# A two-block float32 transformer step on one core: the first job gets four column tiles, the first retention job runs ahead of its layer norm, and the last projection is computed token by column

## The chip, the cores and the metric

The kernel runs on one core of a Trainium2 chip. Times are device microseconds (us) of the whole program. A run is compared by the median of its executions; the profile shows one execution. TensorE is PE, VectorE DVE, ScalarE ACT, GpSimd POOL, and SyncE (SP) only starts transfers.

## The reference, cut to what matters

256 tokens of width 2048 pass through two blocks, all in float32. The parts that the change touches:

```python
h = rms_norm(x, norm_mix[l]); proj = h @ w_in[l]       # first block: four mixers side by side
kv = a_kv.reshape(B, T, 6, NSA_KV_HEADS, HEAD_DIM)      # kv[:, :, 0], kv[:, :, 1]: compressed keys and values
dq, dk, dv = jnp.split(d_cols, 3, axis=-1)              # of the stick-breaking attention
...
x = x + (silu(h @ w_ffn_gate[l]) * (h @ w_ffn_up[l])) @ w_ffn_down[l]
...
# second block: attention layer, then retention layer, each closed by
x = layer_norm(ALPHA * x + mixer(x), gain, bias)        # mean and variance over the 2048 columns of a token
# retention_mixer
proj = h @ w_in                                         # q, k (8 heads of 256), v, g (8 heads of 512)
q, k = rope(q), rope(k); o = chunk_retention(q, k, v, log_g, strict)
return (head_group_norm(o) * silu(g)) @ w_out           # 4096 -> 2048
```

The layer norm ahead of the retention is ln0 below, the one at the end ln1.

## The kernel before, in words

Activations are kept transposed: tile k holds columns 128k to 128k+127 on the partitions and the 256 tokens along the row. Every product is made of split operands: a value is a rounded part (hi) and the remainder (lo), both of a rounded float32 type. An activation tile is [hi | lo], 128x512 (names xA, xB, og, act). A weight unit is 128x1024, loaded by one SP transfer of 512 KB into wf (four buffers); ACT rounds it to wh (L374) and DVE subtracts, wl = wf - wh (L387). `prefetch` keeps wh three units and `low` keeps wl two units ahead of TensorE.

A job is one group of output columns over all rows of the weight. In a T job (`job_T`) the weights are stationary: each pair of a weight row block k and a column tile m takes one 512-column matmul with wh (hi and lo at once, L449) and one 256-column matmul with wl (L450); the result lies column by token. The variant `one` uses three 256-column matmuls (L446, L447, L450). In an N job (`job_N`) the activations are stationary, each row block and token half takes three 512-column matmuls (L473 to L475), and the result lies token by column.

The order of everything is written out: the body issues job after job, and between pairs `S.adv` lets a scheduler step the waiting tasks (generators), so that the evacuations, norms and attention parts are issued among the matmuls. Every engine works off its instructions in the order of issue. The jobs in order: kcvc, aq, ak, av, four dqk, dv, cv, ... (w_in), w_out, the FFN, then the attention's kv, q, g and four ao (output projection, four column tiles each), then for the retention rqk0 (q and k of head 0, four tiles), rv0, then rqk, rv and rg of the heads, and four ro (output projection).

Three places matter. At the **start** x arrives as eight transfers of 256 KB (two tiles each, xr) mixed with the weight units; each tile is scaled and split by ACT (L512) and DVE (L514).

At **ln0** the evacuation `ev_res` adds an ao tile to the residual (L1376, L1378). `LN.add` sums tiles 0 to 7 on POOL; that mean, spread by a matmul with ones (lp, L1293), is subtracted from every tile as a shift (L1297); `stat` squares the tiles on ACT (L1321) and adds them and their squares on POOL (L1322, L1324) into lns and lnq. `sums` adds over partitions by one-column matmuls (pcs, L1343), and `finish` takes mean, variance and rsqrt with some dozen small DVE operations, spreads them by matmuls with ones (lpb L1359, lpn L1367) and hands them to `apply0`, which normalises 16 tiles and splits them into x3 (xB tiles). Only then can rqk0 begin. The last ao job uses two additional buffers of wh and wl and the `one` form.

At the **end**, four T jobs ro feed ln1, which ends in the same `finish`; then the 16 tiles are normalised and leave in 16 transfers, as a 2048 x 256 array.

## Time and profile before

| | us |
|---|---|
| median of three runs | 2307.68 (2307.23 to 2321.01) |
| the profiled execution, own time | 2322.28 |
| its span, first to last instruction | 2320.5 |
| TensorE busy in the span | 2276.0 (98%) |
| VectorE / ScalarE / GpSimd busy | 1532.2 (66%) / 1141.5 (49%) / 414.8 (18%) |
| mean granted TensorE clock | 0.991 of full speed |
| DMA traffic | 408.55 MB, mean 176 GB/s |

The profiled execution lies 0.6% above the median and 0.05% above the slowest of the three runs. Busy time of TensorE comes from modelled ends, so the number of matmuls times the spacing of their starts says more than the 98%.

### The profile page before, as it was taken

How to read it: one execution, taken by the hardware profiler on the slowest of the kernel's cores; microseconds unless marked ns; L12 is line 12 of the kernel's file. 1: busy time of each engine (PE TensorE's matmuls, PEld its weight loads, DVE VectorE, ACT ScalarE, POOL GpSimd, SP SyncE). 2: the span in 40 equal slices, each digit the busy share in tenths (PEclk: the TensorE clock that was granted, in tenths of full speed). 3: DMA queues.
4: the chain of work that ended last, by engine and by line, in shares of the span. 5: the costliest groups of instructions: out<-in, count | busy, mean ns of one | idle time of the engine just before them, and what ended most of it. 6: DMA issues, size and time to landing. Idle time of an engine off the chain costs nothing.

```text
span 2320.5 us, 33510 instructions
## 1 busy us (share of the span) xinstructions
PE 2276.0 (98%) x12755; PEld 1963.9 (85%) x12755; DVE 1532.2 (66%) x2372; ACT 1141.5 (49%) x1690; POOL 414.8 (18%) x406
## 2 busy tenths in 40 slices
PE   8999999999999999999999999999999999999997
PEld 7877888888888888888888888888888888888887
DVE  6666697655555555555558898777677676776464
ACT  5457545544443344444445556455444544446343
POOL 2224331111100011110012222650000000001061
PEclk9999999999999999999999999989999999999998
DMA  7643455565565566666555454444655555556553
GB/s 251 227 150 112 122 187 180 195 190 187 182 192 188 177 189 189 188 185 191 183 190 181 146 156 153 156 168 160 185 168 175 179 172 187 169 173 189 188 168 114
DMA packets 114657, 408.55 MB, mean 176 GB/s; under 512 B 12882, under 2 KB 15186, under 8 KB 114368
## 3 DMA queue, kind: packets, MB, share of 16 engines
q1 hardware_dynamic: 113184, 400.80, 54.9%
q0 software_dynamic: 1168, 5.53, 0.7%
q8 instruction: 100, 1.64, 0.3%
q14 instruction: 61, 0.50, 0.1%
q10 hardware_dynamic: 144, 0.08, 0.0%
HBM read 404.24 MB, written 4.21 MB: 176 GB/s over the span
## 4 chain that ended last, share of the span: by engine, by line
PE 83%; DVE 5%; POOL 3%; issue 2%; ACT 1%; DMA 0%; POOLq 0%; ACTq 0%; DVEq 0%
PE st L449 41%; PE st L450 22%; PE st L473 5%; PE st L474 4%; PE st L475 4%; DVE wl L387 2%; POOL xr L1297 1%; PE mO L1809 1%; PE st L446 1%; PE st L447 1%; PE mA L854 1%; PE mS L1782 0%; POOL lnq L1324 0%; POOL lny L1649 0%; PE mO L835 0%
## 5 line engine op out<-in xcount | busy, mean ns | idle before, releaser
L387 DVE TENSOR_TENSOR wl<-wf,wh 128x1024 fp32r<-128x1024 f32 (+1 forms) x750 | 949.5, 1275 | 301.1 <-ACT wh L374 299.8
L374 ACT ACTIVATE wh<-wf 128x1024 fp32r<-128x1024 f32 (+1 forms) x750 | 788.4, 1055 | 698.9 <-PE st L449 440.9
L449 PE MATMUL st<-xA,wh 128*128 128x512 f32 x2144 | 768.3, 402 | 8.0 <-DVE xA L514 6.7
L450 PE MATMUL st<-xA,wl 128*128 128x256 f32 x2272 | 640.5, 282 | 2.8 <-DVE wl L387 2.8
L449 PE MATMUL st<-xB,wh 128*128 128x512 f32 x1536 | 548.7, 400 | 4.6 <-DVE xB L1655 2.1
L449 PEld LDWEIGHTS st<-xA,wh 128*128 128x128 f32 x2144 | 404.4, 189 | 107.5 <-DVE xA L514 6.7
L450 PEld LDWEIGHTS st<-xA,wl 128*128 128x128 f32 x2272 | 432.0, 190 | 4.2 <-DVE wl L387 4.1
L450 PE MATMUL st<-xB,wl 128*128 128x256 f32 x1536 | 432.0, 281 | 0.0
L449 PEld LDWEIGHTS st<-xB,wh 128*128 128x128 f32 x1536 | 290.4, 189 | 75.5 <-DVE xB L1655 3.2
L450 PEld LDWEIGHTS st<-xB,wl 128*128 128x128 f32 x1536 | 291.8, 190 | 1.1
L449 PE MATMUL st<-act,wh 128*128 128x512 f32 x704 | 248.8, 399 | 0.0
L450 PE MATMUL st<-act,wl 128*128 128x256 f32 x704 | 197.7, 281 | 0.0
L474 PE MATMUL st<-wl,xB 128*128 128x512 f32 x448 | 174.8, 390 | 1.0 <-DVE wl L387 1.0
L473 PE MATMUL st<-wh,xB 128*128 128x512 f32 x448 | 175.4, 392 | 0.0
L475 PE MATMUL st<-wh,xB 128*128 128x512 f32 x448 | 174.5, 389 | 0.0
L449 PEld LDWEIGHTS st<-act,wh 128*128 128x128 f32 x704 | 132.3, 188 | 33.1
L663 DVE TENSOR_TENSOR evs<-st,evt 128x256 f32<-128x256 f32 x110 | 46.2, 423 | 149.9 <-ACT evt L661 149.8
L450 PEld LDWEIGHTS st<-act,wl 128*128 128x128 f32 x704 | 133.0, 189 | 0.0
L1210 POOL TENSOR_TENSOR evs<-evs,R 128x256 f32<-128x256 f32 x44 | 32.4, 737 | 487.3 <-DVE evs L663 487.3
L1753 POOL TENSOR_TENSOR rm<-qkr,c 128x512 f32<-128x512 f32 x16 | 32.5, 2032 | 456.7 <-DVE qkr L1687 451.7
L474 PEld LDWEIGHTS st<-wl,xB 128*128 128x128 f32 x448 | 84.2, 188 | 17.9 <-DVE wl L387 1.9
L475 PEld LDWEIGHTS st<-wh,xB 128*128 128x128 f32 x448 | 84.1, 188 | 17.8
(426 smaller groups left out, 2604.8 us busy)
## 6 DMA issues: line engine op xcount, KB each, us to landing
wf<-in_w_c SPq DMA_DIRECT2D x264, 512.0 KB, 4.2
wf<-in_w_e SPq DMA_DIRECT2D x256, 512.0 KB, 3.9
wf<-in_w_d SPq DMA_DIRECT2D x112, 512.0 KB, 3.6
wf<-in_w_a SPq DMA_DIRECT2D x84, 512.0 KB, 3.8
wf<-in_w_b SPq DMA_DIRECT2D x32, 512.0 KB, 4.0
xr<-in_xT SPq DMA_DIRECT2D x16, 256.0 KB, 5.4
wf<-in_w_a SPq DMA_DIRECT2D x5, 420.0 KB, 4.1
dr<-d POOLq DMA_DIRECT2D x1, 2048.0 KB, 9.7
```

What stands on the lines that cost most here:

```text
L374: ACT.activation(wh[q][:, :n], wf[q][:, :n], AF.Copy)
L387: V.tensor_tensor(wl[q][:, :n], wf[q][:, :n], wh[q][:, :n].bitcast(F32), OP.subtract)
L446: PE.matmul(ps[m][:, :T], hv[:, cs], x[:, :T], start=kk == 0, stop=False)
L447: PE.matmul(ps[m][:, :T], hv[:, cs], x[:, T:], start=False, stop=False)
L449: PE.matmul(ps[m], hv[:, cs], x, start=kk == 0, stop=False)
L450: PE.matmul(ps[m][:, :T], lv[:, cs], x[:, :T], start=False, stop=kk == K - 1)
L473: PE.matmul(p, xh, h[:, o:o + n], start=kk == 0, stop=False)
L474: PE.matmul(p, xh, l[:, o:o + n], start=False, stop=False)
L475: PE.matmul(p, xl, h[:, o:o + n], start=False, stop=kk == K - 1)
L663: V.tensor_tensor(s, p[:, :T], t, OP.add)
L1210: G.tensor_tensor(s, s, R2, OP.mult)
L1753: G.tensor_tensor(m, x[:, ::-1], rsn.rearrange("p (a t) -> p a t", a=2), OP.mult)
```

## The change

**First job.** kcvc takes the first dqk job's two tiles with it: four tiles, two row blocks per unit (eight units in the place of four and four). Unit 0 is loaded and split in halves, and x's first transfer goes between its halves on the SP queue. Ten matmuls of ones stand at the head of TensorE's order. The splits of x from tile 6 on become a task.

**ln0 and rqk0.** The shift is the mean of the first four tiles (NS = 4), begun one job earlier. Each finished, not yet normalised tile is multiplied by its gain and split into xg = [hi | 4 columns | lo], where the four columns hold gain and bias, hi and lo. rqk0 multiplies xg (`ext`: 260, 256 and 258 columns), and its evacuation `ev_first` applies the norm to the four results: the first extra column sums give W·gain and W·bias, and with rm (rsqrt) and lpn (-mean·rsqrt) the result is W·xg·rm + (W·gain)·lpn + W·bias. `norm0` and `apply0` run as tasks beside rqk0; rv0 and the later jobs read the normalised x3. `one` and the additional buffers go. Closing phase 3 and loading c4 move into rv0's first evacuation. `decay` moves into the FFN.

**ro and the end.** The four ro jobs become N jobs, in the last one's last unit ordered by token half. The residual is added up, transposed (32 transposes) and copied by tasks; `bn_stats` runs on each 512 columns of a token half. The end has bn_aggr, rsqrt, 12 matmuls of ones, two transposes, six two-row matmuls that spread bias and mean term, and eight output transfers of 256 KB on two queues; the output is 256 x 2048.

```diff
-    job("a", "T", allk, [(w, cat([kv(0, g), kv(1, g)])) for g in range(2)], 4, "kcvc")
+    job("a", "T", allk, [(w, cat([kv(0, g), kv(1, g)])) for g in range(2)] + dq(0), 2, "kcvc")
...
-    for i in range(4):
-        dqk(i)
+    for i in (2, 1, 3):
+        job("a", "T", allk, dq(i), 4, ("dqk", i))
...
-        job("e", "T", rows, [("ret_w_out_2", P * (4 * m + j) + ar(P)) for j in range(4)], 2, ("ro", m))
+        job("e", "N", rows, [("ret_w_out_2", 512 * m + ar(512))], 2, ("ro", m))
...
+            for c in halves(q, n):
+                nc.sync.dma_start(wf[q][:, c], src[:, c])
+                if q == 0 and then:
+                    then.pop()()
...
+                if ext:
+                    PE.matmul(ps[m][:, :T + 4], hv[:, cs], x[:, :T + 4], start=kk == 0, stop=False)
+                    PE.matmul(ps[m][:, :T], hv[:, cs], x[:, T + 4:], start=False, stop=False)
+                    PE.matmul(ps[m][:, :T + 2], lv[:, cs], x[:, :T + 2], start=False, stop=kk == K - 1)
...
+    for k, c in enumerate(halves(0, n)):
+        ACT.activation(wh[0][:, c], wf[0][:, c], AF.Copy)
         x = newx("A", k)
         run(split(x, xr[k], g1[:, k:k + 1]))
         xA.t[k] = x
+        V.tensor_tensor(wl[0][:, c], wf[0][:, c], wh[0][:, c].bitcast(F32), OP.subtract)
...
+    for z in (1, 2):
+        run(splits(2 * z, 2 * z + 2))
+        prefetch(z + 1)
+    tX = S.add(splits(6, 16))
...
+    def gain(k):
+        if k >= 10:
+            yield 4
+        x = newg(k)
+        g = lng[0][:, k:k + 1]
+        ACT.activation(x[:, :T], xr[k], AF.Copy, scale=g)
+        G.tensor_copy(x[:, T:T + 4], cgb[:, k])
+        yield 2
+        V.scalar_tensor_tensor(x[:, T + 4:], xr[k], g, x[:, :T].bitcast(F32), OP.mult, OP.subtract)
+        xg.t[k] = x
...
+    def norm0():
+        yield 4
+        ln0.head()
+        ln0.sums(ln0.s, ln0.q, True)
+        yield 1
+        yield from ln0.finish()
...
+    ln0.begin()
+    for mm in range(1, 4):
+        job_T(take(), og, ev_res(ln0, mm), 2)
...
+    def ev_first(m, p):
+        S.drain(tap[0])
+        gb = small(2)
+        V.tensor_reduce(gb, p[:, T:T + 4].rearrange("p (a b) -> p b a", a=2), AX.X, OP.add)
+        q = qkr[(0, w)][:, s]
+        V.tensor_tensor(q, p[:, :T], ln0.rm[1], OP.mult)
+        V.scalar_tensor_tensor(q, ln0.rm[2], gb[:, 0:1], q, OP.mult, OP.add)
+        ACT.activation(q, q, AF.Identity, bias=gb[:, 1:2])
...
+    job_T(take(), xg, ev_first, ext=True)
...
+            V.scalar_tensor_tensor(y, res.pop((mm, tt)), ALPHA, p, OP.mult, OP.add)
+            V.bn_stats(bs[tt][:, mm], y)
...
+        job_N(take(), og, ev_ro(mm), mm == 3)
...
+    for m, tt in order[2:]:
+        add[(m, tt)] = p = st()
+        PE.matmul(p, nT[tt][:2, :], gr[:2, 512 * m:512 * m + 512], start=True, stop=True)
+    for n, (m, tt) in enumerate(order):
+        y = y5[tt][:, m]
+        if m == 3:
+            V.tensor_tensor(y, y, gb[:, 512 * m:512 * m + 512], OP.mult)
+            V.tensor_tensor(y, y, ob, OP.add)
+        else:
+            V.scalar_tensor_tensor(y, y, r[:, tt:tt + 1], add[(m, tt)], OP.mult, OP.add)
+        (ACT if n % 2 else nc.sync).dma_start(out[tt * P:tt * P + P, 512 * m:512 * m + 512], y)
```

**The order at three places.** A row is a line of the kernel, an operation, the tile it writes, the tiles it reads, its shape; numbers behind a name tell buffers apart. VectorE at the start of the program, before (L514 makes the lo half of an x tile, L387 the lo of a weight unit):

```order
L514 SCALAR_TENSOR_TENSOR xA_125<-xr_90,vec_72,xA_125 128x256
L514 SCALAR_TENSOR_TENSOR xA_128<-xr_90,vec_72,xA_128 128x256
L514 SCALAR_TENSOR_TENSOR xA_131<-xr_92,vec_72,xA_131 128x256
L514 SCALAR_TENSOR_TENSOR xA_134<-xr_92,vec_72,xA_134 128x256
L387 TENSOR_TENSOR wl_139<-wf_88,wh_123 128x1024
```

Four x tiles, then the first weight unit. The same place after the change (L532 is L514, L637 the halves of unit 0, L393 is L387):

```order
L532 SCALAR_TENSOR_TENSOR xA_136<-xr_99,vec_72,xA_136 128x256
L637 TENSOR_TENSOR wl_134<-wf_100,wh_133 128x512
L532 SCALAR_TENSOR_TENSOR xA_141<-xr_99,vec_72,xA_141 128x256
L637 TENSOR_TENSOR wl_134<-wf_100,wh_133 128x512
L532 SCALAR_TENSOR_TENSOR xA_145<-xr_106,vec_72,xA_145 128x256
L532 SCALAR_TENSOR_TENSOR xA_148<-xr_106,vec_72,xA_148 128x256
L532 SCALAR_TENSOR_TENSOR xA_155<-xr_110,vec_72,xA_155 128x256
L532 SCALAR_TENSOR_TENSOR xA_158<-xr_110,vec_72,xA_158 128x256
L393 TENSOR_TENSOR wl_165<-wf_104,wh_153 128x1024
```

Unit 0's two halves stand right behind the first two x tiles; unit 1's lo stands behind four more x tiles, of x's second and third transfer.

TensorE between the last pair of the last ao job and rqk0, before (pcs sums, lpb and lpn spread the norm, st<-xB is rqk0):

```order
L450 MATMUL st_14332<-xA_13755,wl_14496 128x256
L1343 MATMUL pcs_14356<-ones_74,xr_13761 128x1 x2
L1343 MATMUL pcs_14356<-ones_74,lnu_14588 128x1 x2
L1343 MATMUL pcs_14356<-ones_74,xr_13761 128x1 x2
L1343 MATMUL pcs_14356<-ones_74,lnu_14608 128x1 x2
L1359 MATMUL lpb_14633<-lndg_14631,ones_74 128x256
L1367 MATMUL lpn_14641<-lndg_14631,ones_74 128x256
L449 MATMUL st_14643<-xB_14657,wh_14494 128x512
```

Nothing of rqk0 stands ahead of the norm. After the change, two pieces of TensorE's order inside rqk0 (st<-xg), behind its ninth pair and behind its nineteenth:

```order
L449 MATMUL st_14608<-xg_14140,wh_14536 128x260
L450 MATMUL st_14608<-xg_14140,wh_14536 128x256
L451 MATMUL st_14608<-xg_14140,wl_14616 128x258
L1405 MATMUL pcs_14661<-deps_77,ones_74 128x1 x2
L1439 MATMUL pcs_14661<-ones_74,lns_13602 128x1 x2
L1439 MATMUL pcs_14661<-ones_74,lnq_13603 128x1 x2
...
L451 MATMUL st_14610<-xg_14146,wl_14618 128x258
L1459 MATMUL lpb_14707<-lndg_14705,ones_74 128x256
L449 MATMUL st_14611<-xg_14146,wh_14612 128x260
```

The sums and the spreading matmuls now stand among rqk0's own matmuls. VectorE over the same stretch after the change (L1478 and L1480 evacuate the last two ao tiles, L1418 adds squares, L1699 makes the lo half of an xg tile, L1446 is the first small operation of the norm):

```order
L1478 TENSOR_TENSOR xr_13822<-st_14378,xr_13822 128x256
L1480 TENSOR_TENSOR xr_13822<-st_14378,xr_13822 128x256
L1418 TENSOR_TENSOR lnq_13603<-lnq_13603,lnt_14592 128x256
L1699 SCALAR_TENSOR_TENSOR xg_14595<-xr_13794,vec_72,xg_14595 128x256
L1418 TENSOR_TENSOR lnq_13603<-lnq_13603,lnt_14600 128x256
L1699 SCALAR_TENSOR_TENSOR xg_14604<-xr_13794,vec_72,xg_14604 128x256
L393 TENSOR_TENSOR wl_14616<-wf_14447,wh_14536 128x1024
L393 TENSOR_TENSOR wl_14618<-wf_14474,wh_14612 128x1024
L393 TENSOR_TENSOR wl_14651<-wf_14496,wh_14614 128x1024
L1699 SCALAR_TENSOR_TENSOR xg_14643<-xr_13822,vec_72,xg_14643 128x256
L1446 TENSOR_SCALAR sm_14675<-pcs_14661 128x2
```

The lo of rqk0's second unit (wl_14616) stands behind the last evacuation and four more operations, and the norm's small operations stand behind three weight units.

## Rows read from the trace of the kernel before

**Rows 1.** The page: the chain of work that ended last, shares of the span by engine.

```profile
PE 83%; DVE 5%; POOL 3%; issue 2%; ACT 1%; DMA 0%; POOLq 0%; ACTq 0%; DVEq 0%
```

**Rows 2.** The waits of TensorE, the row of lpb: waiting line, releasing line, us in total, times, longest.

```profile
PE lpb L1359 <- ACT lndg L1362: 6.1, 2, 3.0
```

**Rows 3.** The timeline of the first 14 us: start, length, engine, line, operation, count, and in brackets the idle time ahead of it with its releaser.

```profile
4.68 1.06 ACT L374 ACTIVATE wh<-wf 128x1024 fp32r<-128x1024 f32 x1 [2.23 <-DMA wf<-in_w_a]
...
6.71 0.79 PE L449 MATMUL st<-xA,wh 128*128 128x512 f32 x1 [6.71 <-DVE xA L514]
7.77 1.22 DVE L387 TENSOR_TENSOR wl<-wf,wh 128x1024 fp32r<-128x1024 f32 x1
8.89 1.06 ACT L374 ACTIVATE wh<-wf 128x1024 fp32r<-128x1024 f32 x1 [1.55 <-DMA wf<-in_w_a]
...
9.04 0.58 PE L450 MATMUL st<-xA,wl 128*128 128x256 f32 x1 [1.54 <-DVE wl L387]
...
10.07 0.63 PE L449 MATMUL st<-xA,wh 128*128 128x512 f32 x1
...
10.71 0.63 PE L449 MATMUL st<-xA,wh 128*128 128x512 f32 x1
...
13.05 0.28 PE L450 MATMUL st<-xA,wl 128*128 128x256 f32 x1
```

**Rows 4.** A window of the same stretch: from and to, its length, busy time of each engine with the number of instructions, granted TensorE clock, DMA share, GB/s.

```profile
5.00:10.00 5.00, 1.75 (x4) 1.15 (x5) 2.82 (x5) 3.44 (x7) 0.00 (x0) 1.00 1.05 384
```

**Rows 5.** Windows with the same columns (PE, PEld, DVE, ACT, POOL, clock, DMA share, GB/s): ao jobs 1 to 3 with the end of job 0; the gap ahead of rqk0; rqk0; rv0; the four ro jobs; the end.

```profile
1423.20:1526.30 103.10, 97.83 (x608) 87.47 (x607) 78.23 (x129) 50.80 (x86) 51.70 (x53) 0.97 0.52 169
1526.30:1535.65 9.35, 4.19 (x22) 3.20 (x21) 5.55 (x23) 3.69 (x7) 2.48 (x4) 0.58 0.01 2
1535.65:1561.10 25.45, 25.45 (x129) 21.76 (x130) 22.66 (x39) 19.20 (x32) 19.62 (x21) 0.89 0.40 125
1561.10:1586.00 24.90, 23.87 (x111) 19.30 (x110) 17.30 (x20) 12.41 (x15) 2.53 (x2) 1.00 0.63 221
2116.30:2301.50 185.20, 184.24 (x1169) 165.29 (x1168) 104.16 (x111) 78.30 (x106) 49.82 (x52) 1.00 0.53 167
2301.50:2320.50 19.00, 3.91 (x22) 2.92 (x20) 11.17 (x39) 9.68 (x20) 6.90 (x10) 0.62 0.32 110
```

**Rows 6.** The timeline around the holes in the last ao job (columns as in Rows 3).

```profile
1501.79 1.03 ACT L1321 ACTIVATE lnt<-xr 128x256 f32<-128x256 f32 x3 [1.79 <-POOL xr L1297]
...
1504.69 0.58 PE L446 MATMUL st<-xA,wh 128*128 128x256 f32 x1 [2.77 <-ACT wh L374]
...
1506.43 0.58 PE L450 MATMUL st<-xA,wl 128*128 128x256 f32 x1 [0.94 <-DVE wl L387]
```

**Rows 7.** The timeline of the gap ahead of rqk0 (columns as in Rows 3).

```profile
1528.45 0.16 DVE L1350 TENSOR_SCALAR sm<-pcs 128x2 f32<-128x2 f32 x1 [1.50 <-PE pcs L1343]
...
1531.00 0.29 DVE L1364 TENSOR_SCALAR lndg<-ident,sm 128x128 f32<-128x128 f32 x1
...
1531.45 1.22 PE L1359 MATMUL lpb<-lndg,ones 128*128 128x256 f32 x2 [3.04 <-ACT lndg L1362]
...
1535.65 0.80 PE L449 MATMUL st<-xB,wh 128*128 128x512 f32 x1 [2.12 <-DVE xB L1655]
```

**Rows 8.** The chain of work that ended last, three stretches in order of time: start, share, engine, tile, line, count. From the first to the second row lie 32 pairs.

```profile
2200.03 0.24 PE st L449
...
2211.34 0.23 PE st L449
2211.69 0.45 PE lp L1293 x2
...
1525.23 0.79 PE pcs L1343 x8
```

**Rows 9.** The timeline of TensorE in a job of 280 columns (start, length, line, shape).

```profile
49.95 0.29 PE L474 MATMUL st<-wl,xA 128*128 128x280 f32 x1
50.08 0.29 PE L475 MATMUL st<-wh,xA 128*128 128x280 f32 x1
```

**Rows 10.** The timeline of TensorE in an N job of 512 columns; six matmuls lie from the first row to the second.

```profile
1830.05 0.39 PE L475 MATMUL st<-wh,xB 128*128 128x512 f32 x1
...
1831.41 0.39 PE L475 MATMUL st<-wh,xB 128*128 128x512 f32 x1
```

**Rows 11.** Groups of instructions by line and shape: count, busy us, mean ns of one, idle time ahead of them.

```profile
L387 DVE TENSOR_TENSOR wl<-wf,wh 128x1024 fp32r<-128x1024 f32 x744 | 942.7, 1276 | 296.9 <-ACT wh L374 295.6
L514 DVE SCALAR_TENSOR_TENSOR xA<-xr,vec,xA 128x256 fp32r<-128x256 f32 x32 | 18.6, 631 | 6.4 <-ACT xA L512 6.4
L1376 DVE TENSOR_TENSOR xr<-st,xr 128x256 f32<-128x256 f32 x32 | 13.5, 421 | 22.9 <-PE st L450 22.9
L1297 POOL TENSOR_TENSOR xr<-xr,lnc 128x256 f32<-128x256 f32 x22 | 25.8, 1190 | 5.6 <-ACT lnc L1294 5.6
L1860 POOL TENSOR_TENSOR xr<-xr,lnrm 128x256 f32<-128x256 f32 x10 | 6.9, 729 | 8.7 <-ACT lnrm L1365 8.7
L1827 PE MATMUL mT<-ident,on 128*128 128x128 f32 x64 | 9.6, 272 | 0.0
L1786 DVE SCALAR_TENSOR_TENSOR dm<-mS,dm 128x512 f32<-128x512 f32 x8 | 5.5, 692 | 9.1 <-PE mS L1782 9.0
```

**Rows 12.** The timeline of the end (columns as in Rows 3).

```profile
2310.78 6.50 ACT L1865 ACTIVATE xr<-xr,vec 128x256 f32<-128x256 f32 x13 [0.16 <-DVE xr L1864]
```

More of the change, by code (lines that the diff above doesn't have):

```diff
@@ L586, in load_x @@
         return r
+    pw_ = mB()
+    for _ in range(10):
+        PE.matmul(pw_[:, :P], ones, ones, start=True, stop=True)
     ACT.dma_start(vec, a["vecs"])
-    load(1)
-    xr = load_x(lambda z: load((z + 1) // 2 + 1))
+    x0 = s2("xr", (P, 2, T))
+    then.append(lambda: nc.sync.dma_start(x0, a["xT"][0]))
+    load(2)
+    xr = load_x(lambda z: load(min(z + 2, WFB)), x0)
     G.dma_start(ident, a["ident"])
@@ L609, in body, with splits @@
         xA.t[k] = x
-        if k % 4 == 3 and k < 12:
-            prefetch(k // 4 + 2)
+        V.tensor_tensor(wl[0][:, c], wf[0][:, c], wh[0][:, c].bitcast(F32), OP.subtract)
+    del wf[0]
+    pos["sp"] = pos["lo"] = 1
+    def splits(a, b):
+        for k in range(a, b):
+            x = newx("A", k)
+            yield from split(x, xr[k], g1[:, k:k + 1])
+            xA.t[k] = x
+            yield 1
[3 more added lines that the diff above has]
+    tX = S.add(splits(6, 16))
+    for k in range(6, 16):
+        xA.by[k] = tX
     def norm1():
+        yield 10
         acc, accb = s1("acc"), s1("accb")
@@ L674, in body @@
     zT = s2("zT", (P, 2, T))
+    dqk = [[s2("dqk", (P, 2, T)) for _ in range(2)] for _ in range(2)]
     zb = q1.tile([P, 2, NCMP, 32], F32, name="zb")
@@ L915, in body @@
     tQK = S.add(task_qk())
-    dqk = [[s2("dqk", (P, 2, T)) for _ in range(2)] for _ in range(2)]
     def ev_dqk(i):
@@ L935, in body @@
     tA = S.add(task_A())
-    for i in range(2, 4):
-        job_T(take(), xA, ev_dqk(i))
+    job_T(take(), xA, ev_dqk(3))
     dv = [None, None]
@@ L1242, in body @@
         act = XS(S, HFF)
+        if h:
+            S.add(decay())
         while jq[0]["tag"][0] == "gu":
@@ L1324, in stat @@
                 (G if k < 12 else V).tensor_tensor(self.q, self.q, sq, OP.add)
-                if k == 11:
-                    self.ps = self.pp.tile([P, 512], F32, name="pcs", tag=self.tag)
-                    for tt in range(2):
-                        PE.matmul(self.ps[:, 2 + tt:3 + tt], ones, deps, start=tt == 0, stop=False,
-                                  skip_group_check=True)
+                if self.done:
+                    pass
+                elif k == 11:
+                    self.head()
                 elif k == 13:
@@ L1630, in body @@
-    S.add(decay())
-    for mm in range(1, 4):
-        job_T(take(), og, ev_res(ln0, mm), 2, q3 if mm == 3 else None, one=mm == 3)
-    S.drain_all()
-    rm = ln0.finish()
-    x3 = XS(S)
+    cgb = q3.tile([P, 16, 4], F32R, name="cgb")
+    for z, v in enumerate((lng[0], lnb[0])):
+        ACT.activation(cgb[:, :, z], v, AF.Copy)
+        V.tensor_tensor(cgb[:, :, 2 + z], v, cgb[:, :, z].bitcast(F32), OP.subtract)
+    tap = []
+    def norm0():
+        yield 4
+        ln0.head()
+        ln0.sums(ln0.s, ln0.q, True)
+        yield 1
+        yield from ln0.finish()
@@ L1856, in body @@
     S.drain_all()
[L1857 to L1866 removed]
+    mv, r = small(4), small(2)
@@ new lines, in body @@
+    pw_ = pm.tile([P, 512], F32, name="rt", tag="rt", bufs=2)
+    for _ in range(12):
+        PE.matmul(pw_[:, :P], ones, ones, start=True, stop=True)
+    for tt in range(2):
+        V.bn_aggr(mv[:, 2 * tt:2 * tt + 2], bs[tt].rearrange("p a b -> p (a b)"))
+    rsqrt(r, mv[:, 1::2], 1.0, 1e-5, 2)
+    for tt in range(2):
+        V.scalar_tensor_tensor(nm[tt][:, 0:1], mv[:, 2 * tt:2 * tt + 1], -1.0, r[:, tt:tt + 1], OP.mult, OP.mult)
+    pt = pm.tile([P, 512], F32, name="rt", tag="rt", bufs=2)
@@ new lines, in body @@
+    for tt in range(2):
+        PE.transpose(pt[:2, tt * P:tt * P + P], nm[tt], ident)
+    for tt in range(2):
+        y = y5[tt][:, 3]
+        ACT.activation(y, y, AF.Identity, scale=r[:, tt:tt + 1], bias=nm[tt][:, 0:1])
+        if tt == 0:
+            for z in range(2):
+                ACT.activation(nT[z][:2, :], pt[:2, z * P:z * P + P], AF.Copy)
+    order = [(m, tt) for m in (3, 0, 1, 2) for tt in range(2)]
+    add = {}
+    for m, tt in order[2:]:
+        add[(m, tt)] = p = st()
+        PE.matmul(p, nT[tt][:2, :], gr[:2, 512 * m:512 * m + 512], start=True, stop=True)
```

368 lines of the change are left out of this document (222 added, 146 removed).

## The prediction

> **What bounds the kernel now.** I read the chain of work that ended last first: 83% of the span lies on TensorE [rows 1], so time is won only where it has fewer or cheaper matmuls, or where it stands still. Next the waits: lpb, the spreading of a norm, waits twice, 6.1 us together [rows 2]. Last the windows of the stretches that the change touches [rows 5] and their timelines. The prices on TensorE: 32 pairs take 11.31 us, .3534 a pair [rows 8]; six 512-column matmuls of an N job take 1.36 us, so a triple takes .68 [rows 10]. In both forms the same product costs .707 (two pairs) or .68.
>
> **Start.** Before, the first matmul starts at 6.71, its second waits for wl until 9.04, then pairs start .64 apart (10.07 and 10.71) and the eighth ends at 13.05 to 13.3 [rows 3]. After, the first two x tiles and half units come earlier, so eight pairs (two row blocks of four tiles) can run from about 6.5 on. But the ninth needs wl of unit 1, which DVE has behind x tiles 2 to 5. x's third transfer ends 2.25 MiB into the SP queue; 1.5 MiB were in at 8.89 [rows 3], and .79 MB more at 384 GB/s [rows 4] puts it at 10.9. Then come ACT's and DVE's parts of two tiles, 2 x .63 [rows 11] on DVE, and 1.28 for wl: 13.4 or so. By then before has done nine pairs and runs at the full clock; after has done eight and stood still behind them, for 1 to 2 us. In the gap ahead of rqk0, where TensorE also stood, the granted clock was .58 [rows 5]. I take +1.5 us; the bounds are 0 (wl early enough) and +3.5 (hole and half clock in full). The other moves in the first block (order of dqk, splits as a task, `decay` in the FFN) lie beside a busy TensorE and put nothing new on it; 0, with 2 us either way in the range.
>
> **ln0, rqk0, rv0: what goes.**
> - The gap ahead of rqk0, 9.35 us [rows 5]. Of it 2.55 are 13 small DVE operations (1528.45 to 1531.00) and the rest the spreading and the first normalised tile, until 1535.65 [rows 7].
> - rqk0 itself: 25.45 us for 64 pairs, which cost 22.6; its granted clock is .89, and .58 in the gap ahead of it [rows 5]. Full 2.4 GHz throughout saves 2.8.
> - The last ao job: the stretch of 256 pairs took 103.1 [rows 5] against 90.5 by price. POOL had not finished the shift (L1297), so ACT's squares and behind them the rounding of weights came late: TensorE waited 2.77 and .94 [rows 6], and the granted clock of the stretch is .97 [rows 5], 3 us less than full. Of the 12.6 in excess .45 is lp [rows 8], 1.2 the sums (next point), and of the other 11 I take 8.0: the two holes, the clock, and some 1.3 of smaller ones and of the `one` form; 3 stay with the older jobs. The change takes the cause away in part: the shift starts a job earlier and the squares are tasks.
> - The sums of tiles 14 and 15 behind the job, 1.2.
> - rv0: 24.90 with 23.87 of it busy [rows 5], 1.0.
>
> Together 22.4.
>
> **ln0, rqk0, rv0: what comes.**
> - Wider matmuls: 774 columns in three instructions where a pair had 768 in two. 280 columns in this type start .13 after one another [rows 9]; three of these would be .39, +.03 a pair and 2.0 on 64; by columns alone it is 0. I take .6.
> - The norm's matmuls within rqk0: 12 of one column at .10 and two spreads at .45 [rows 8], 2.1.
> - A late DVE. Behind the last ao matmul it has, in order, two evacuation adds (.42 each), two lnq adds, two xg halves (.63) and then wl of rqk0's second unit (1.28) [rows 11]; with .58 for an lnq add, about the .6 of the operations around it, that is 4.5 us, while eight pairs cover 2.9 plus .2: a stall of 1.4. The spread lpb stands behind the nineteenth pair, due at 9.5 us; its input waits for two more units, two xg halves and 13 small operations (2.55 [rows 7]): 10.9, another 1.4. TensorE is in order, so rqk0's pairs behind lpb wait with it. lpn adds .3. Sum 3.1; 0 if POOL and ACT run ahead, 6 if xg of the last tiles is later still.
> - The third ao job, whose first units are rounded by an ACT that also squares and makes xg: .7 (0 to 4).
> - rv0 starts with closing the phase and the load of c4: .4 (0 to 1).
>
> Together 6.9, so this stretch gives -15.5, between -9 and -20. apply0's work (16 tiles, POOL, DVE, ACT) is hidden by rqk0 and due only at rv0, whose first row blocks need x3's first tiles: uncovered it would cost at most the old gap's last part, 4.2 (1531.45 to 1535.65 [rows 7]).
>
> **ro.** Before 185.2 [rows 5]. After, 256 triples at .682 are 174.5. The 32 transposes, at .15 with modelled ends [rows 11], are at most 4.8; back to back less, 4.0. 178.5: -6.7 (-5.5 to -8). Evacuations (an add and bn_stats, 1.4 together) come only eight times, on a DVE that is busy 104 of 185 us [rows 5].
>
> **End.** Before 19.0 [rows 5]; ACT's last tile ends at 2317.28 [rows 12], 3.2 us ahead of the span's end. After the last matmul: the add at .69 and bn_stats, as wide and so put at the same [rows 11], with the hand-over 1.65; 13 small operations 2.55, so 4.2; the norm's mean term 4.6; ACT's tile, .5 for 256 columns in the old end [rows 12], and four DVE operations of .69 [rows 11] until 8.0. Meanwhile transposes, a copy and six two-row matmuls of 512 columns, which cost twice the .45 of a 256-column one [rows 8]: from 6.3 to 11.7, the last add .7 more, 12.4, and 3.2 for the last transfer: 15.6. With the idle time of TensorE ahead of them, the clock may be at 1.2 GHz (granted .62 over the old end, [rows 5]): three of the six then cost double, 18.3; all six, 21. I take 16.5: -2.5, between -3.4 and +2.
>
> **Sum.** +1.5 - 15.5 - 6.7 - 2.5 = -23.2. The profiled execution would take 2322.3 - 23.2 = 2299.1. It is 14.6 above the median; nothing in that difference belongs to the stages touched, so the median goes from 2307.7 to 2284.5, 1.0% less. 1% is about what a measurement of this kernel can tell from no change.
>
> **The rivals.**
> *All covers hold.* DVE is never late, no hole at the start: start 0, ln0 -20, ro -7.5, end -3.6, in all -31: 2276.5. For it: in the gap DVE and ACT were busy 5.55 and 3.69 of 9.35 us [rows 5], so part of what I charge is waiting. Against it: DVE works 22.66 of rqk0's 25.45 us [rows 5], with fewer tasks than it will have.
> *POOL and DVE hold each other up.* POOL's subtraction L1297 took 1190 ns where DVE is busy beside it, and the like multiplication L1860 took 729 in the end, where DVE does short operations on one SBUF input [rows 11]. In the new stretch both work on SBUF pairs all the time: subtractions, lns and lnq adds, xg halves. If the last tiles' chain has six such operations at .46 more, it is 2.8 later, DVE's queue with weights behind it as well: holes of 5.9 us in place of 3.8, and the clock behind them lowered as in the last ao job, 3.4. ln0 gives -9.3 to -10 and the whole -17: 2290.7. The Trainium skill, page "SBUF — State Buffer", section "Who interferes with whom", says that a VectorE instruction with two SBUF inputs and a GpSimd one that reads SBUF take a shared port pair in turn, the second standing still until the first is done. The two durations of POOL agree with that; what DVE loses no row here shows.
> *The extended matmuls are not taken at the fast rate.* rqk0's 260 and 258 columns have an odd shape; if they ran at the price of full float32, .225 per 128x256 pass and two passes (.45, [rows 8]) and not .12, then 128 of them cost .33 more each, +42 us: with the other terms 2326.5, slower than before. It decides if the two wide ones of a pair cost over .18 more each, as 128 times that is the 23 us. Against it: 280 columns ran at .13 [rows 9].
> *The change doesn't do what it says.* If rqk0 still began behind the norm, the gap would stay; the order of TensorE has the norm's matmuls behind nine and nineteen of its pairs, so no chance of its own.
>
> **How the numbers follow.** Forecast .48, all covers .28, POOL and DVE .20, slow matmuls .04. The range runs from 2274 (all covers, 2.5 lower for the first block) to 2300: POOL and DVE with the upper bounds of start and end, 3 to 4.5 each. Only slow matmuls and a tenth at either side lie outside. Faster by over 1% is below 2284.6: all of all covers, nearly half of the forecast, which lies on that line: .51. Slower by over 1% is .04, the rest .45.
>
> **What would show it.** After: in the first 14 us a wait of st for wl at the ninth pair, 1 to 2 us; no gap over 3 us between ao and rqk0; rqk0 at 23 to 27 us with lpb and wl as its waits, granted clock near 1; the ro stretch at 178 to 180; 15 to 19 us behind the last ro matmul. The forecast is wrong if a hole of several us appears in the third ao job or in rv0's beginning, where POOL's chain ends and x3 is due, or if the spread matmuls at the end run at 1.2 GHz.

## The result and the profile after

The changed kernel takes 2326.23 us (median of seven, 2323.55 to 2328.99) against 2307.68: a ratio of 1.0073 with a 95% interval of 1.0055 to 1.0092. It is 0.7% slower, where 2284.5 with a range of 2274 to 2300 was forecast.

One thing must be said first: executions of the kernel before fall into two groups, near 2307 and near 2321, and the profile ahead of the prediction is one of the second; the stages below are compared with a later profile of the first group (b0_before, span 2303.3, own time 2305.15).

The windows of the changed kernel that answer to [rows 5] (same columns): ao jobs 1 to 3 with job 0, rqk0, a gap behind it, rv0, the four ro jobs, the end.

```profile
1434.30:1528.97 94.67, 93.43 (x533) 80.72 (x531) 78.22 (x104) 53.90 (x97) 57.35 (x62) 1.00 0.53 173
1528.97:1556.90 27.93, 27.02 (x210) 26.66 (x208) 24.22 (x51) 18.20 (x32) 16.40 (x21) 0.94 0.42 133
1556.90:1562.00 5.10, 0.16 (x3) 0.04 (x1) 4.95 (x11) 3.69 (x7) 5.06 (x6) 1.00 0.32 103
1562.00:1585.83 23.83, 23.83 (x96) 19.22 (x97) 17.73 (x27) 14.70 (x22) 5.48 (x5) 0.93 0.69 224
2125.50:2305.40 179.90, 179.90 (x802) 147.40 (x801) 95.44 (x85) 70.56 (x74) 34.25 (x25) 1.00 0.56 179
2305.40:2323.50 18.10, 11.89 (x40) 5.87 (x38) 10.91 (x28) 1.83 (x4) 0.00 (x0) 0.71 0.31 116
```

The gap ahead of rqk0 is gone, as forecast, but a gap of 5.1 us stands behind it. The waits of TensorE (columns as in [rows 2]) show where it comes from, and three waits in the first block that are longer than before (1.2, 1.2 and 1.3 us there):

```profile
PE st L483 <- DVE xB L1795: 4.9, 1, 4.9
PE mA L893 <- POOL pr L920: 4.3, 4, 2.3
PE st L484 <- DVE wl L393: 3.1, 1, 3.1
PE mA L865 <- DVE sm L862: 2.7, 2, 2.3
...
PE mA L1094 <- DVE gq L1089: 2.3, 1, 2.3
```

L1795 evacuates rqk0. L865 and L893 belong to the first block's attention, L1094 to its gelu. The account by stage, from the start of each job's first matmul in the two traces (before is b0_before):

| stretch | changed minus before, us | forecast |
|---|---|---|
| start to the job dv | -2.4 | +1.5 |
| dv to the second wo job (first block's attention) | +14.3 | 0 |
| from there to the third ao job (FFN, attention layer) | +14.0 | 0 |
| from there to rqk0's start | -17.5 | part of -15.5 |
| rqk0 to the end of rv1 | +14.9 | part of -15.5 |
| rqk, rv, rg of the other heads | +1.5 | 0 |
| four ro jobs | -3.9 | -6.7 |
| end | -0.9 | -2.5 |
| sum of the spans, 2303.3 to 2323.5 | +20.2 | -23.2 |

So the gains came, smaller, and three losses stand beside them: in the first block's attention, in the FFN and the attention layer, and behind rqk0. The FFN alone, in windows of the same work (kernel before, then changed; columns as in [rows 5]):

```profile
420.22:1153.27 733.05, 733.05 (x4232) 646.37 (x4231) 417.49 (x534) 345.00 (x463) 73.20 (x92) 1.00 0.59 190
```

```profile
433.02:1177.14 744.12, 744.12 (x4232) 648.74 (x4231) 423.87 (x574) 347.32 (x466) 72.70 (x92) 1.00 0.59 187
```

As many matmuls, no idle time in either, the granted clock 1.00 in both, and 11.1 us between them.

### The profile page after: what moved, and what is told of

Its sections match the earlier page's. It is cut to its first block, busy times and chain, and to the rows that moved or that the text cites. A ratio compares the mean times of both kernels' runs of the same rounds, so it can differ in the third digit from the quotient of the medians.

```text
span 2323.5 us, 32707 instructions
## 1 busy us (share of the span) xinstructions
PE 2287.2 (98%) x12411; PEld 1955.9 (84%) x12411; DVE 1534.0 (66%) x2365; ACT 1136.0 (49%) x1665; POOL 403.2 (17%) x381
## 4 chain that ended last, share of the span: by engine, by line
PE 85%; DVE 6%; ACT 1%; issue 1%; POOL 1%; POOLq 0%; DVEq 0%
PE st L460 38%; PE st L461 20%; PE st L483 7%; PE st L484 7%; PE st L485 7%; DVE wl L393 2%; PE mO L1935 1%; PE mS L1908 0%; PE mA L904 0%; PE st L2050 0%; PE mT L1953 0%; PE mO L885 0%; POOL pr L920 0%; PE mA L893 0%; PE mP L1600 0%
## 5 line engine op out<-in xcount | busy, mean ns | idle before, releaser
L393 DVE TENSOR_TENSOR wl<-wf,wh 128x1024 fp32r<-128x1024 f32 x749 | 953.5, 1283 | 297.5 <-ACT wh L383 295.5
L383 ACT ACTIVATE wh<-wf 128x1024 fp32r<-128x1024 f32 x749 | 788.5, 1055 | 714.2 <-PE st L460 391.4
L460 PE MATMUL st<-xA,wh 128*128 128x512 f32 x2616 | 935.1, 400 | 3.8 <-ACT wh L383 2.0
L461 PE MATMUL st<-xA,wl 128*128 128x256 f32 x2616 | 738.1, 282 | 2.1 <-DVE wl L393 2.0
L460 PE MATMUL st<-xB,wh 128*128 128x512 f32 x872 | 312.4, 399 | 3.2 <-DVE evs L706 2.6
L461 PE MATMUL st<-xB,wl 128*128 128x256 f32 x872 | 245.8, 282 | 0.0
L460 PEld LDWEIGHTS st<-xB,wh 128*128 128x128 f32 x872 | 164.7, 189 | 42.7 <-DVE evs L706 3.2
L461 PEld LDWEIGHTS st<-xB,wl 128*128 128x128 f32 x872 | 164.9, 189 | 0.2
L483 PE MATMUL st<-wh,xA 128*128 128x512 f32 (+2 forms) x400 | 156.2, 391 | 4.9 <-DVE xB L1795 4.9
L484 PE MATMUL st<-wl,xA 128*128 128x512 f32 (+2 forms) x400 | 152.4, 381 | 3.1 <-DVE wl L393 3.1
L485 PE MATMUL st<-wh,xA 128*128 128x512 f32 (+2 forms) x400 | 152.3, 381 | 0.0
```

The lines of the kernel that those rows point to most:

```text
L383: ACT.activation(wh[q][:, :n], wf[q][:, :n], AF.Copy)
L393: V.tensor_tensor(wl[q][:, :n], wf[q][:, :n], wh[q][:, :n].bitcast(F32), OP.subtract)
L460: PE.matmul(ps[m], hv[:, cs], x, start=kk == 0, stop=False)
L461: PE.matmul(ps[m][:, :T], lv[:, cs], x[:, :T], start=False, stop=kk == K - 1)
L483: PE.matmul(p, xh, h[:, o:o + n], start=kk == 0, stop=False)
L484: PE.matmul(p, xh, l[:, o:o + n], start=False, stop=False)
```

## The experiments

**A profile of the usual execution.** b0_before is the kernel before, unchanged.

> The kernel before, unchanged, for a profile of an execution at its usual 2307 us; the profile shown ahead of the prediction was one of 2322. If the 15 us lie in a few waits, its jobs differ from the profile shown at single places (the waits at 292 us, at 1502 us) and the rest is equal to 0.3 us. If the price of a matmul pair differs, the difference grows evenly over all jobs, about 0.65%, .3511 in place of .3534 a pair.

Measured: 2308.22 (2305.15 to 2310.28), profile 2303.3. Its span is 17.1 us shorter than that of the profile of [rows 1 to 12], and 13.8 of these lie in the FFN: a gate and up job (32 pairs) takes 11.093 us in place of 11.310, a down job (88 pairs) 30.51 in place of 31.10, each kind of job equal to some 10 ns. A pair is .3467 or .3534. The waits are nearly the same in both. The second branch expected the difference evenly over all jobs, and it isn't: the last two wo jobs ahead of the FFN take 22.19 us in both profiles, the rqk jobs of heads 2 to 7 take 11.31 in both. So the price of a pair has levels, two of them within one execution here, and the execution that the prediction started from was on the upper one in the FFN.

**The first block's attention.** u1_two_tiles takes the merged first job back, u2_raw_first puts the dqk job with the compressed weights first:

```diff
# u1_two_tiles
-    job("a", "T", allk, [(w, cat([kv(0, g), kv(1, g)])) for g in range(2)] + dq(0), 2, "kcvc")
+    job("a", "T", allk, [(w, cat([kv(0, g), kv(1, g)])) for g in range(2)], 4, "kcvc")
...
-    for i in (2, 1, 3):
+    for i in range(4):
...
# u2_raw_first
-    for i in (2, 1, 3):
+    for i in (1, 2, 3):
```

> The changed kernel with the first job as before: two tiles, four row blocks a unit, the four dqk jobs in their old order behind av; halves, transfers and ten matmuls of ones at the start stay as changed. Theory: the merged job puts 11 us of dqk work ahead of everything that the attention of the first block hangs on, so its chain comes 13 us later than the jobs that hide it, and the waits between 200 and 370 us (10 us in the trace) are the price; without it 9 to 13 us less than the changed kernel, and the job wo 1 starts under 357 us in place of 364.7. Rival: the new order of the x transfers and the splits as a task do it; then 0 to 2 us less.

> The changed kernel with the dqk jobs in the order 1, 2, 3: the one that carries the compressed weights (raw) stands first behind av, so the task of the compressed branch starts 11 to 12 us earlier. If that task is what comes late, 6 to 11 us less than the changed kernel. If it is the task of the queries and keys, which starts behind av and isn't moved by this edit, 0 to 3 us less.

u1: 2326.90, no gain, where 9 to 13 us were expected. But TensorE's waits in it (the first fence, columns as in [rows 2]) have L865 and L893 at 1.0 us each, as before the change: the jobs cu, bch and bb take 39.2, 65.3 and 25.1 us as before (39.2, 65.1, 25.0) and not 42.5, 72.9 and 26.9. In their place the start waits six times for x tiles (L532), which two tiles a row block use up twice as fast, and for the first norm (pb L565), and the last dqk job holds 20 small attention matmuls again (15.3 us in place of 12.2), so the job dv begins 13.0 us later. u2 (a wait of it in the second fence): 2321.33, 5 us less, where 6 to 11 were expected; L865 and L893 are at 1.1 us each here too, the second wo job starts at 358.9 in place of 364.7, and a wait for the queries' transposes (L955) has come.

```profile
PE st L460 <- DVE xA L532: 5.7, 6, 2.6
...
PE pb L565 <- DVE dg L562: 2.8, 1, 2.8
```

```profile
PE mA L955 <- DVE qn L947: 2.1, 1, 2.1
```

The stretch from the job dv to the second wo job in b0_before, the changed kernel and u2 (windows, columns as in [rows 5]):

```profile
129.19:352.70 223.51, 216.08 (x1175) 177.38 (x1174) 164.96 (x332) 133.45 (x239) 85.94 (x65) 1.00 0.44 141
```

```profile
126.82:364.68 237.86, 225.22 (x1196) 183.38 (x1195) 169.96 (x350) 134.11 (x240) 86.05 (x66) 0.98 0.42 137
```

```profile
134.84:358.89 224.05, 217.07 (x1175) 177.79 (x1174) 164.83 (x332) 133.54 (x239) 85.95 (x65) 1.00 0.42 142
```

The changed kernel's 14.3 us can be added up: 5.6 are the three longer waits; for 10.2 us of the stretch the granted clock is .50, which costs about half of that (an estimate); and some 3 are the attention matmuls, 21 more in the window, that before stood in the last dqk job. The width of the tiles has no part in it: p2_before516 below, with the wider tiles and the old first job, takes 224.0 us here, and c2_xg_own, with narrow tiles and the new first job, 241.0.

What follows: the attention's task of the compressed branch starts with the raw job (the dqk job that carries the compressed weights), and that job begins 12.8 us later than before (95.8 against 83.0), because dqk's first tiles now lie in the merged job ahead of everything. Its softmax and products then reach TensorE when the jobs that should hide them are running out: from the raw job's start to that of cu the kernel before and u1 have 113 us, u2 has 118, the changed kernel 98. The theory holds for the waits, not for the sum: both versions pay part of it elsewhere, and of the 7.8 us that u2's dqk jobs grew some 4 are the wait and a lowered clock behind it, and 3 the 20 attention matmuls, back in the last dqk job.

**Behind rqk0.** The timeline of the changed kernel around the gap (columns as in [rows 3]):

```profile
1555.81 3.36 POOL L1742 TENSOR_TENSOR xr<-xr,lnrm 128x256 f32<-128x256 f32 x3
...
1556.78 0.28 PE L451 MATMUL st<-xg,wl 128*128 128x258 f32 x1
...
1556.85 0.41 DVE L1743 TENSOR_TENSOR xr<-xr,lpn 128x256 f32<-128x256 f32 x1
...
1559.37 1.75 DVE L393 TENSOR_TENSOR wl<-wf,wh 128x1024 fp32r<-128x1024 f32 x1
...
1561.44 0.41 DVE L1795 TENSOR_TENSOR xB<-st,lnrm 128x256 f32<-128x256 f32 x1
...
1562.00 0.74 PE L483 MATMUL st<-wh,xA 128*128 128x512 f32 x1 [4.94 <-DVE xB L1795]
```

rqk0's last matmul is at 1556.78, and its first evacuation at 1561.4: VectorE works through apply0's operations first, and these wait for GpSimd's multiplications (L1742, three in 3.36 us). rv0's result needs the evacuated bank. The trace of rv1 has the second place: VectorE does head 1's rope (L1880) and head 0's group norm (L1940, some ten small operations from L504 on, L1946) in a row, and the weight unit behind them comes at 1623:

```profile
1614.66 1.78 DVE L1880 TENSOR_TENSOR qkr<-qkr,c 128x512 f32<-128x512 f32 x1
1616.37 0.68 DVE L1940 BATCH_NORM_STATS2 sm<-mO 128x6 f32<-128x512 f32 x1
...
1621.14 1.52 DVE L1946 TENSOR_SCALAR on<-mO,sm 128x512 f32<-128x512 f32 x2
...
1623.18 1.22 DVE L393 TENSOR_TENSOR wl<-wf,wh 128x1024 fp32r<-128x1024 f32 x1
```

```diff
# u3_apply_paced, in apply0
-            yield 1 + (k % 3 > 0)
+            yield 3
# p3_rope_now, in task_rope
-        if h == 0:
-            yield 8
```

> The changed kernel with apply0 stepped more slowly (three steps a tile in place of one or two), so that nine tiles and not twelve stand ahead of rqk0's first evacuation on VectorE. Theory: the 5.2 us of TensorE's wait at 1557 us are rqk0's evacuation standing in VectorE's queue behind apply0, which GpSimd paces at 1.1 us an operation; then the wait falls to 1 to 3 us, the lowered clock behind it goes, and the run is 3 to 6 us shorter. Rival: GpSimd's chain itself is what sets the end, since rv0 needs x3 anyway; then the wait is only cut into pieces within rv0 and the sum changes by under 1.5 us.

> The changed kernel without the eight steps that head 0's rope task waits. Theory: the 3.5 us of TensorE's wait at 1621 us and the lowered clock behind it come from head 0's group norm (14 small and 3 large operations) falling onto head 1's rope on VectorE, ahead of a weight unit, because phase 4 opens 24 us later than before; 4 to 6 us earlier they part, the wait falls under 1.5 us, and the run is 3 to 6 us shorter. Rival: the load of c4, 5.5 us, then sets the begin of the rope, and head 0 stays late: under 1.5 us change.

u3: 2318.93, 7 us less, more than expected; rv0 starts at once at the full clock. The first window is the end of rqk0, the second is rv0, both without idle time and with a clock of 1.00:

```profile
1551.70:1557.07 5.37, 5.37 (x48) 5.37 (x46) 5.30 (x11) 4.44 (x7) 4.46 (x4) 1.00 0.60 202
1557.07:1579.24 22.17, 22.17 (x99) 17.91 (x97) 20.50 (x37) 18.13 (x29) 11.03 (x10) 1.00 0.58 196
```

p3: 2320.00, 6 us less; the wait in rv1 is gone, since the group norm is done by 1611.7 and head 1's rope starts at 1615. Both theories hold: TensorE waited for VectorE's order, and GpSimd's data was no bound for rv0.

**The price of a pair.** Every job of the FFN costs a little more in the changed kernel, 11.24 and 31.09 us. Beside decay's small VectorE operations the change leaves one trace there, the memory plan: the 16 tiles A0 to A5 and B6 to B15 became 516 columns wide for xg's four extra columns. Seven kernels ask for the cause:

```diff
# p1_pad520: the changed kernel
-            return pxs.tile([P, 516], dt, name="x" + t[0], tag="x" + t)[:, :512]
+            return pxs.tile([P, 520], dt, name="x" + t[0], tag="x" + t)[:, :512]
...
# p2_before516: the kernel before, all 16; w1_a_wide: A0 to A5 alone; w2_b_wide: B6 to B15 alone
-        return pxs.tile([P, 512], F32R, name=f"x{n}", tag=f"x{n}{k}")
+        w = 516 if f"{n}{k}" in GT else 512
+        return pxs.tile([P, w], F32R, name=f"x{n}", tag=f"x{n}{k}")[:, :512]
# s1_shift16: 16 bytes ahead of the tiles; s2_behind256: the same behind them with 64 columns, 256 bytes
+    psh = top.enter_context(tc.tile_pool(name="psh", bufs=1))
+    psh.tile([P, 4], F32, name="dummy")
# c2_xg_own: the changed kernel, all x tiles 512 columns
-        return pxs.tile([P, 516], F32R, name="xg", tag="x" + GT[k])
+        return q3.tile([P, 516], F32R, name="xg", tag=f"xg{k}")
```

> The changed kernel with its 16 wider activation tiles at 520 columns (a multiple of 32 bytes) in place of 516 (a multiple of 16); nothing else. In the trace every FFN job of the changed kernel costs the same little more than before: 11.24 in place of 11.09 us for the 64 matmuls of a gate and up job, 31.09 in place of 30.51 for a down job, 11 us over the FFN, whose code is not changed. Theory: the place of the tiles in the memory sets it; then these jobs fall to 11.09 to 11.15 and 30.5 to 30.7 and the run is 6 to 13 us shorter. If 32 bytes are not enough, or the place is not the cause, 11.24 and 31.09 stay and the run changes by under 1.5 us.

> The kernel before with the same 16 activation tiles 516 columns wide, of which it uses 512; order and work are the same. If the place of the tiles sets the price of a matmul pair: gate and up jobs at 11.24, down jobs at 31.09, and 8 to 15 us more than before (2316 to 2322). If not: 2306 to 2310, the jobs at 11.09 and 30.51.

> The kernel before with 16 unused bytes ahead of the activation tiles, so that all of them and all that lies behind them move by 16 bytes, and their distance stays 2048. If a start that isn't on a multiple of 64 bytes sets the price of a pair: 11.24 and 31.09 us for the FFN jobs, 2320 to 2323. If it is the distance of the tiles: 11.09 and 30.51, 2306 to 2310.

> The kernel before with 256 unused bytes behind the activation tiles: these stay where they were, and the later pools, the FFN's hidden tiles among them, move by 256 bytes, as far as the 16 wider tiles move them. If each job's price hangs on the place of its own moving tile: gate and up jobs at 11.09, down jobs at 31.09, 2312 to 2314. If on the activation tiles alone: both low, 2306 to 2310. If on any shift of the pools: both high, 2320 to 2323.

> The kernel before with only tiles A0 to A5 at 516 columns. The gate and up jobs read A tiles, the down jobs read none of the widened ones. If a job pays for the distance of the tiles that it reads, and the state of the matmul stream stays as long as nothing interrupts it: gate and up jobs at 11.24 and down jobs at 31.09, 2318 to 2323. If only the sum of the shift counts: 11.09 and 30.51, 2306 to 2310.

> The kernel before with only tiles B6 to B15 at 516 columns, which no FFN job reads. If the distance of the tiles read sets the price: 11.09 and 30.51, 2306 to 2311. If any change of the memory plan does: 11.24 and 31.09, 2318 to 2323.

> The changed kernel with the un-normalised tiles xg in buffers of their own, in the third phase's pool, so that all activation tiles are 512 columns wide again. If the wider tiles cost the changed kernel what they cost the kernel before (14.5 us, most of it in the FFN): 2310 to 2314, FFN jobs at 11.09 and 30.51. If the FFN's higher price comes from something else in the change: 2324 to 2328.

| kernel | median, us | gate/up job, us | down job, us |
|---|---|---|---|
| b0_before | 2308.22 | 11.093 | 30.51 |
| changed | 2326.23 | 11.240 | 31.09 |
| p1_pad520 | 2327.48 | 11.240 | 31.09 |
| p2_before516 | 2322.83 | 11.240 | 31.09 |
| s1_shift16 | 2305.90 | 11.093 | 30.51 |
| s2_behind256 | 2307.41 | 11.093 | 30.51 |
| w1_a_wide | 2324.74 | 11.240 | 31.09 |
| w2_b_wide | 2310.32 | 11.093 | 30.70 |
| c2_xg_own | 2309.93 | 11.093 | 30.51 |

The FFN as a whole says the same: 745.1 us in p2_before516 and 734.1 in c2_xg_own, beside the 744.1 and 733.1 above, at a granted clock of 1.00 and without idle time in all four.

Sixteen bytes more between tiles, with the same order, work and transfers, cost the kernel before 14.6 us (2322.83 against 2308.22), and the changed kernel loses 16.3 when they go (2326.23 to 2309.93). The first of these figures is one between the two groups of executions: in the measurement that p2_before516 belongs to, the kernel before itself had 14 executions at 2307 to 2313 us and 15 at 2319 to 2326, and p2's ten all lie at 2322 to 2324. For w1_a_wide the contrast is plain: both of its executions are in the upper group (2323.77 and 2325.72), none of the 19 of the kernel before beside it is above 2313. So the wider tiles make the rule of what the kernel before does now and then; tiles of 512 columns do not rule it out, as one of c2_xg_own's ten executions (2323.21) shows.

It takes the A tiles, which the gate and up jobs read. Wider B tiles alone leave the time as it was within the noise (2310.32 against 2308.64 of the kernel before beside it), though a down job then takes 30.70. A start 16 bytes off does nothing to the FFN, 520 columns don't help, and shifting what lies behind the tiles does nothing there either. For the gate and up jobs that fits the distance of the tiles read. Whether it is the distance itself, or that six tiles have another distance than the other ten, no run tells, as none widens all 16 A tiles. Two things don't fit that reading: the down jobs read none of the widened tiles and pay too, and the kernel before has an upper price in some executions with the same plan (31.10 in the profile of [rows 1 to 12]). The single matmuls show a pattern: on the lower level the pair is 230 + 117 ns throughout, on the upper one a period of three pairs (240 + 120, 236 + 114, 232 + 118 in a down job). Why, no run here tells.

**ro and the end alone.** r1_ro_end is the kernel before with N jobs for ro and the new end only (the diff's hunks on ro, res_task, ev_ro and the end).

> The kernel before with one part of the change alone: the four output jobs token by column, their tasks, and the new end. No tile is wider, the start and the norm are as before. By the prediction's terms -6.7 (four jobs) and -2.5 (end): 9 us less, 2298 to 2300. By the two traces, where the four jobs went from 183.6 to 179.8 and the end from 19.0 to 18.2: 4 to 5 us less, 2302 to 2304. The FFN jobs should stay at 11.09 and 30.51 us, as no tile moves there; if the changed weight layout or the code moves them to 11.24 and 31.09, 2313 to 2318.

Measured: 2302.94, ratio 0.9978 (0.9959 to 0.9996). Its windows of the four jobs and the end, and those of b0_before behind them:

```profile
2103.21:2280.90 177.69, 177.69 (x802) 147.15 (x801) 93.87 (x85) 70.57 (x74) 37.25 (x25) 1.00 0.54 180
2280.90:2300.90 20.00, 13.70 (x40) 6.54 (x38) 11.17 (x28) 1.83 (x4) 0.00 (x0) 0.65 0.28 105
```

```profile
2100.60:2284.25 183.65, 182.31 (x1168) 164.91 (x1167) 104.17 (x111) 78.24 (x106) 50.12 (x52) 1.00 0.53 169
2284.25:2303.30 19.05, 4.02 (x23) 3.03 (x21) 11.16 (x39) 9.67 (x20) 6.91 (x10) 0.57 0.32 110
```

The jobs gain 6.0, the end loses 0.9.

**Everything together.** c1_combo is the changed kernel with u2, u3, p3 and p1; c3_parts leaves the first-job part out altogether and takes the rest with u3, p3 and c2.

> The changed kernel with four edits together: dqk order 1, 2, 3; apply0 three steps a tile; no eight steps ahead of head 0's rope; tiles at 520 columns. If the causes add up: -5.5 (order), -7 (apply0), -3 to -6 (rope), -6 to -13 (tiles): 2294 to 2305 us, under the kernel before (2307 to 2309). If the tiles give nothing: 2307 to 2311.

> The change without its first-job part, with xg in buffers of their own, apply0 three steps a tile and head 0's rope without its eight steps: the ln0 and rqk0 part as forecast, and the ro part. From the stage tables: start and first block as before (0), FFN as before (0), ln0 to the end of rv1 -11 to -15 (forecast -15.5), ro -6, end 0 to +1: 2288 to 2293, under all kernels so far. If the late evacuation and the late group norm come back in the new place: 2295 to 2302.

c1: 2312.42, above the branch "tiles give nothing", which the 520 columns did. The gains do not add up in full: from rqk0 to the end of rv1 u3 is 8.6 us shorter than the changed kernel, p3 6.2, and c1 10.3 and not 14.7, as a job of rqk1 now takes 16.0 us in place of 11.3, with a wait of 2.4 for a weight unit in it. c3: 2290.31 (2288.20 to 2290.45), ratio 0.9913 (0.9896 to 0.9929), the fastest of all. Its windows, from the first ao job on (ao jobs, rqk0, rv0, rqk1 and rv1):

```profile
1409.70:1504.40 94.70, 92.62 (x533) 80.39 (x532) 78.31 (x104) 53.77 (x97) 56.47 (x62) 1.00 0.53 173
1504.40:1531.60 27.20, 25.78 (x211) 25.27 (x210) 24.37 (x50) 18.20 (x30) 15.83 (x19) 1.00 0.48 156
1531.60:1553.50 21.90, 21.90 (x98) 17.83 (x97) 20.23 (x37) 17.89 (x29) 11.00 (x10) 1.00 0.56 167
1553.50:1609.70 56.20, 52.88 (x270) 44.73 (x270) 41.12 (x60) 24.37 (x33) 6.80 (x4) 0.97 0.56 185
```

From the first ao job to the end of rv1 it takes 200.0 us, b0_before 211.0 (1408.7 to 1619.75): the ln0 part is worth 11.0 with those waits out, with a wait of 3.3 for a weight unit left in the fourth window. With -6.0 for ro (177.7 us) and +1.3 for the end (20.3) that makes -15.7, and the spans differ by 14.8, so start, first block and FFN together are within 1 us of before. Beside the changed kernel's trace, c3's is 11.3 us shorter up to the second wo job, 13.7 from there to the third ao job, and 8.9 from rqk0 to the end of rv1: the three losses.

## Why the prediction was wrong, point by point

**The base.** The step "nothing in that difference belongs to the stages touched" was true but for some 1.5 us of the ro jobs (185.2 us there, 183.7 in b0_before), and missed the point: 13.8 of the 17.1 us between the two profiles were the price of the pairs in the FFN, .3534 against .3467. The changed kernel is on an upper level in its profile and, by its seven times, in every execution. The sum has no term for the FFN and the attention layer, and their code is all but unchanged; leaving them at 0 was the dearest mistake. From the second wo job to the third ao job the changed kernel takes 14.0 us more, p2_before516, which has the wider tiles alone, 13.4, and c2_xg_own, which has all but these, 0.2.

**Start.** The hole was where it was said to be, at the ninth pair, but it had two parts: that pair's first matmul waited 2.0 us for its wh, which the forecast left out, and the second 2.0 us for wl (from 12.83 on in VectorE's order; forecast 13.4 for its end, measured 14.1). Behind it the pairs ran .64 apart, at a granted clock of .50 from 12.4 to 19.2. Against that, the eight pairs ahead of it ran .353 apart, not .64 as before. The ten matmuls of ones stand ahead of these eight, and that they are the reason fits c3_parts, which has none and whose first pairs lie .64 apart again; but c3 leaves out the rest of the first-job part too, so it is not shown for them alone. TensorE's timeline of the changed kernel:

```profile
3.77 1.91 PE L609 MATMUL mB<-ones 128*128 128x128 f32 x8
...
7.00 0.39 PE L460 MATMUL st<-xA,wh 128*128 128x512 f32 x1
...
7.35 0.40 PE L460 MATMUL st<-xA,wh 128*128 128x512 f32 x1
...
11.65 0.50 PE L460 MATMUL st<-xA,wh 128*128 128x512 f32 x1 [2.03 <-ACT wh L383]
14.11 0.58 PE L461 MATMUL st<-xA,wl 128*128 128x256 f32 x1 [1.96 <-DVE wl L393]
```

The merged job gives way to the next at 35.98, where in b0_before its two parts add up to 34.65 (22.55 and 12.10 for the first dqk job): +1.3, beside a forecast of +1.5. The size is right by luck, as a longer hole and faster pairs ahead of it cancel. The -2.4 by the job dv is not of the start: 3.1 of it are the attention matmuls that left the last dqk job and come back behind dv.

**"Put nothing new on it; 0."** The other moves in the first block cost 14.3 behind the job dv, 12 with the 2.4 ahead of it. The step looked at what is added to TensorE and not at when the tasks start that must be hidden: the raw job starts 12.8 us later.

**ln0, what goes.** Of the 22.4 expected, 18.6 lay ahead of rqk0's start (the gap, the last ao job, the sums), and .7 was to come back in the third ao job; from that job to rqk0's start 17.5 went. That stands. The stall for rqk0's second weight unit came (0.9 for 1.4), the one for lpb did not.

**ln0, what comes.** rqk0 itself took 27.9 us; the terms make it 28.5 (25.45 - 2.8 + .6 + 2.1 + 3.1). Here two other terms failed. "apply0's work is hidden by rqk0 and due only at rv0" asked when x3 is needed and not what stands behind apply0 in VectorE's queue: rqk0's own evacuation, 5.1 us and a lowered clock. "rv0 starts with closing the phase, .4 (0 to 1)" priced the load of c4 and not that head 0's rope, and so its group norm, move into head 1's: the rope starts 4 us behind the begin of rqk1 (1589.5 and 1585.8), where in b0_before it starts 21 us ahead of it (1549.1 and 1570.3). That cost a wait of 3.1 us and again the clock. The whole came to -2.6 in place of -15.5; without these two, in c3, -11.0.

**ro.** The term was right: 178.5 was forecast, 177.7 is measured without wider tiles, and 179.9 with them. The gain is 6.0 and not 6.7, as the jobs take 183.7 and not 185.2 in b0_before.

**End.** 16.5 forecast, 18.1 measured, 20.0 in r1, against 19.05 before, so no gain is left beyond what the end varies by. The reason is the one held as a bound: the two-row matmuls run at 1.2 GHz, in part or all. The six of the program are twelve in TensorE's timeline of the changed kernel, 8.55 us together. In its windows (columns as in [rows 5]) the granted clock is 1.00 for the first few, whose starts lie .43 apart, and .50 from 2312.96 on, where they lie .85 apart:

```profile
2309.94 0.38 PE L2039 MATMUL rt<-ident,nm 128*2 128x128 f32 x2 [1.58 <-DVE nm L2036]
2310.85 8.55 PE L2050 MATMUL st<-gr,nT 2*128 2x512 f32 x12 [0.53 <-ACT nT L2045]
```

```profile
2310.85:2312.96 2.11, 2.11 (x5) 1.03 (x6) 2.04 (x4) 0.81 (x2) 0.00 (x0) 1.00 0.00 0
2312.96:2319.40 6.44, 6.44 (x8) 1.99 (x6) 3.93 (x6) 0.00 (x0) 0.00 (x0) 0.50 0.65 244
```

In r1 they lie .85 apart from the second on. The prediction's two cases, 18.3 with half of them slow and 21 with all, come close to both.

**The rivals.** The extended matmuls ran at the fast rate: in the even part of rqk0 three of them start some .36 us behind the three before, where a pair takes .35. The 2326.5 that this rival gave lies 0.3 us from the measured median by chance. GpSimd and VectorE did hold each other up: in the changed kernel's trace L1742 takes .72 to 1.72 us, the like operation alone took 729 ns [rows 11], and the three longest, all near 1.7, are those that begin while a weight subtraction L393 runs on VectorE; L393 loses as well, 1.75 us at 1559.37 against 1.22 at 1623.18. It is part of why apply0 is late, but u3 shows that the order and not GpSimd's speed made the wait. The rule of the Trainium skill that the prediction named (page "SBUF — State Buffer", section "Who interferes with whom") fits these durations. None of the rivals had the mechanisms that decided: the pair's price with wider tiles, the late attention task, and VectorE's order behind rqk0 and in rv1. Slower than before was given .04 for over 1%; 0.7% slower lies in the class "within 1%", and outside the range.
